# Gelu of one half times the other half, in 16 tiles: the rows that a partition owns, interleaved by tile or adjacent in memory

## The chip, the cores and the metric

The kernel runs on one core of a Trainium2 chip. The metric is the device time of a run in microseconds. The time before is the median of three runs, 470.57 us (470.28 to 470.79). A run with the hardware profiler gives the profile.

## What is computed

```
x = randn(32, 512, 2048), float32
x1, x2 = x[..., :1024], x[..., 1024:]
gelu_x1 = 0.5 * x1 * (1 + erf(x1 / sqrt(2)))
return gelu_x1 * x2          # (32, 512, 1024), float32
```

Each row of 2048 numbers (8 KB) becomes a row of 1024 numbers (4 KB). Rows don't depend on one another. There are 32 x 512 = 16,384 rows: 128 MiB (134.22 MB) are read and 64 MiB (67.11 MB) are written.

## The kernel before

The rows are flattened to one list of 16,384 and cut into 16 tiles of 1024 rows. In a tile each of the 128 partitions holds R = 8 rows. L38 and L39 set which rows these are: the list is split as (n p r), so tile n takes 1024 adjacent rows, partition p of it the eight adjacent rows from n x 1024 + p x 8 on. A tile of the input is thus 8 MB of adjacent memory, in which partitions lie 64 KB apart, and a tile of the output 4 MB with partitions 32 KB apart. Each partition's share of a tile is one unbroken piece.

SBUF holds two input tiles (`x_tiles`, L44) and two output tiles (`o_tiles`, L45), used in turn by even and odd tiles. The order of the work is written out by hand:

- `load(i)` (L54 to L59) is issued from ScalarE's queue, one DMA of 8 MB for a tile. Tile 0 alone comes in two DMAs, of rows 0 to 3 and 4 to 7 of each partition. Loads 0 and 1 are issued ahead of the loop (L61, L62).
- For each tile ScalarE applies Gelu in place to the first half of each row (L72), and VectorE multiplies it by the second half into the output tile (L77). Tiles 1 to 14 do this in one instruction each, over 128 x 8192 numbers. The first and the last tile do it in three pieces, of 2, 2 and 4 rows for each partition.
- The result goes out from SyncE's queue: one DMA of 4 MB (L89), or for the first and the last tile two DMAs of 2 MB (L87).
- At the end of the loop's body, load i + 2 is issued (L93) into the buffer that tile i has just used. It waits for the multiply of tile i.

`no_wait` (L47) tells the framework that a dependence is already implied by another wait; it adds no instruction. So there are two DMA queues, ScalarE's with the loads (q10 in the profile) and SyncE's with the stores (q1). Both are worked off by the same 16 DMA engines of the core. ScalarE also computes, so a load that waits for its buffer stands in ScalarE's order ahead of the next Gelu.

Of the kernel before, what the change touches and what calls it, by code (L numbers as in the profile page):

```python
# [1 line left out]

# [4 lines left out]

GELU = mybir.ActivationFunctionType.Gelu


@with_exitstack
def kernel(
    ctx: ExitStack,
    tc: tile.TileContext,
    x: bass.AP,
    out: bass.AP,
):

    nc = tc.nc
    P = nc.NUM_PARTITIONS  # L30

    x_flat = x.flatten_outer_dims()
    out_flat = out.flatten_outer_dims()
    n_rows, dim = x_flat.shape
    half = dim // 2

    R = 8
    x_t = x_flat.rearrange("(n p r) d -> n p r d", p=P, r=R)  # L38
    o_t = out_flat.rearrange("(n p r) d -> n p r d", p=P, r=R)  # L39
    n_tiles = x_t.shape[0]  # L40

    xpool = ctx.enter_context(tc.tile_pool(name="xpool", bufs=1))
    opool = ctx.enter_context(tc.tile_pool(name="opool", bufs=1))
    x_tiles = [xpool.tile([P, R, dim], x.dtype, name=f"x{k}_tile") for k in range(2)]  # L44
    o_tiles = [opool.tile([P, R, half], out.dtype, name=f"o{k}_tile") for k in range(2)]  # L45

    def no_wait(ins, others):  # L47
        for other in others:
            tc.declare_no_dep(ins, other, reason="implied by another wait")

    x_users, o_users = ([], []), ([], [])
    loads = {}

    def load(i):  # L54
        x_tile = x_tiles[i % 2]
        loads[i] = []
        for rows in (slice(0, 4), slice(4, 8)) if i == 0 else (slice(0, 8),):
            dma = nc.scalar.dma_start(out=x_tile[:, rows, :], in_=x_t[i][:, rows, :])  # L58
            loads[i].append(dma.ins)  # L59

    load(0)  # L61
    load(1)  # L62
    for i in range(n_tiles):
        x_tile, o_tile = x_tiles[i % 2], o_tiles[i % 2]
        last = i == n_tiles - 1
        pieces = i == 0 or last
        steps = ((0, 2), (2, 4), (4, 8)) if pieces else ((0, 8),)
        gelus, muls = [], []
        for lo, hi in steps:
            rows = slice(lo, hi)  # L70
            gelu = tc.keep_in_program_order(
                nc.scalar.activation(  # L72
                    out=x_tile[:, rows, :half], in_=x_tile[:, rows, :half], func=GELU
                )
            )
            no_wait(gelu.ins, x_users[i % 2])
            mul = nc.vector.tensor_mul(  # L77
                out=o_tile[:, rows, :],
                in0=x_tile[:, rows, :half],
                in1=x_tile[:, rows, half:],  # L80
            )
            no_wait(mul.ins, loads[i] + x_users[i % 2] + o_users[i % 2])
            gelus.append(gelu.ins)
            muls.append(mul.ins)
            if pieces and hi % 4 == 0:
                part = slice(hi - 4, hi)
                nc.sync.dma_start(out=o_t[i][:, part, :], in_=o_tile[:, part, :])  # L87
        if not pieces:
            nc.sync.dma_start(out=o_t[i], in_=o_tile)  # L89
        x_users[i % 2].extend(gelus + muls + loads[i])  # L90
        o_users[i % 2].extend(muls)
        if i + 2 < n_tiles:
            load(i + 2)  # L93


# [1 line left out]
_INS = ['x']  # L97
_OUTS = [((32, 512, 1024), 'float32')]


# [23 lines left out]
```

## Time and profile before

| what | value |
|---|---|
| median of three runs | 470.57 us (470.28 to 470.79) |
| the profiled execution's own time | 470.61 us |
| its span, from first to last instruction | 468.8 us |
| Gelu over a whole tile, L72, x14 | 7.03 us each |
| multiply over a whole tile, L77, x14 | 8.69 us each |
| a load DMA of 8 MB, from issue to landing, median | 42.2 us |
| a store DMA of 4 MB, from issue to landing, median | 42.4 us |

How to read the profile: the page gives each engine's busy time and its share of the span, then the span in 40 slices with the busy share of the 16 DMA engines in tenths and the rate that they moved in GB/s. For each DMA queue it gives the number of packets, the MB and the time that its packets took, as a share of the time of 16 engines. The chain of waits is followed back from the last instruction: each piece has its start, its length and what it was. A window is a stretch of the span with what each engine did in it. ACT is ScalarE, DVE VectorE, SP SyncE, and L72 is line 72 of the kernel.

### The profile page before, as it was taken

How to read it: one execution, taken by the hardware profiler on the slowest of the kernel's cores; microseconds unless marked ns; L12 is line 12 of the kernel's file. 1: busy time of each engine (PE TensorE's matmuls, PEld its weight loads, DVE VectorE, ACT ScalarE, POOL GpSimd, SP SyncE). 2: the span in 40 equal slices, each digit the busy share in tenths (PEclk: the TensorE clock that was granted, in tenths of full speed). 3: DMA queues.
4: the chain of work that ended last, by engine and by line, in shares of the span. 5: the costliest groups of instructions: out<-in, count | busy, mean ns of one | idle time of the engine just before them, and what ended most of it. 6: DMA issues, size and time to landing. Idle time of an engine off the chain costs nothing.

```text
span 468.8 us, 150 instructions
## 1 busy us (share of the span) xinstructions
DVE 139.5 (30%) x20; ACT 114.2 (24%) x21; POOL 0.2 (0%) x4
## 2 busy tenths in 40 slices
DVE  0330333407033070430704207052070510606142
ACT  1320505041050410505005050140501405023060
POOL 0000000000000000000000000000000000000000
DMA  8999999999999999999999999999999999999998
GB/s 358 447 447 447 414 389 495 403 403 447 481 414 403 447 403 492 403 433 417 492 403 403 447 492 403 403 447 447 447 403 439 411 492 403 403 447 492 403 403 358
DMA packets 5041, 201.33 MB, mean 429 GB/s; under 512 B 561, under 2 KB 561, under 8 KB 561
## 3 DMA queue, kind: packets, MB, share of 16 engines
q10 hardware_dynamic: 2448, 134.22, 66.3%
q1 hardware_dynamic: 2592, 67.11, 33.2%
q14 instruction: 1, 0.00, 0.0%
HBM read 134.22 MB, written 67.11 MB: 429 GB/s over the span
## 4 chain that ended last, share of the span: by engine, by line
DMA 72%; DVE 14%; ACT 12%; ACTq 1%; issue 0%
DMA x_tile<-in_x_dram 72%; DVE o_tile L77 14%; ACT x_tile L72 12%; ACTq L119 0%; ACTq L58 0%
## 5 line engine op out<-in xcount | busy, mean ns | idle before, releaser
L77 DVE TENSOR_TENSOR o_tile<-x_tile 128x8192 f32<-128x8192 f32 (+2 forms) x20 | 139.5, 6985 | 320.7 <-ACT x_tile L72 320.7
L72 ACT ACTIVATE x_tile<-x_tile 128x8192 f32<-128x8192 f32 (+2 forms) x20 | 113.0, 5662 | 339.4 <-DMA x_tile<-in_x_dram 339.4
L72 ACT ACT_TABLE_LOAD x1 | 1.3, 1283 | 2.1 <-issue 2.1
L108 POOL MEMSET const-bfloat16-1.0<- 128x1 bf16 x1 | 0.1, 102 | 0.0
L108 POOL MEMSET const-uint8-127<- 128x1 uint8 x1 | 0.1, 102 | 0.0
L108 POOL MEMSET const-float32-0.0<- 128x1 f32 x1 | 0.1, 99 | 0.2 <-issue 0.2
L108 POOL MEMSET const-float32-1.0<- 128x1 f32 x1 | 0.1, 99 | 0.0
## 6 DMA issues: line engine op xcount, KB each, us to landing
out_dram<-o_tile SPq DMA_DIRECT2D x14, 4096.0 KB, 42.4
x_tile<-in_x_dram ACTq DMA_DIRECT2D x2, 4096.0 KB, 16.8
out_dram<-o_tile SPq DMA_DIRECT2D x4, 2048.0 KB, 18.0
x_tile<-in_x_dram ACTq DMA_DIRECT2D x15, 42.2
```

The source lines that it names most:

```text
L72: nc.scalar.activation(out=x_tile[:, rows, :half], in_=x_tile[:, rows, :half], func=GELU)
L77: mul = nc.vector.tensor_mul(out=o_tile[:, rows, :], in0=x_tile[:, rows, :half], in1=x_tile[:, rows, half:],)
L108: nc = _bacc.Bacc("TRN2", target_bir_lowering=False, num_devices=1)
```

## The change

```
-    x_t = x_flat.rearrange("(n p r) d -> n p r d", p=P, r=R)
-    o_t = out_flat.rearrange("(n p r) d -> n p r d", p=P, r=R)
+    x_t = x_flat.rearrange("(p n r) d -> n p r d", p=P, r=R)
+    o_t = out_flat.rearrange("(p n r) d -> n p r d", p=P, r=R)
```

The list of rows is now split as (p n r): partition p owns the 128 adjacent rows from p x 128 on, and tile n takes eight of them from each partition, those from p x 128 + n x 8 on. A partition's share of a tile is still one unbroken piece of 64 KB in the input and 32 KB in the output. The pieces of neighbouring partitions now lie 1 MB apart in the input and 512 KB apart in the output, where they were 64 and 32 KB apart and touched one another. From tile to tile, each partition's piece moves on by 64 KB in the input and 32 KB in the output. Input and output use the same split, so each result goes to the row it came from. Nothing else in the kernel differs; its lines stand two lines lower, because two blank lines were added (the load's L58 is L60, the Gelu's L72 is L74, the multiply's L77 is L79, the stores' L87 and L89 are L89 and L91).

## The prediction, made before the changed kernel was run

> **What bounds the kernel now.** I read the page first, for busy shares and queues. Its engine table and the row of slices under it say at once which resource is full.
>
> ```profile
> span 468.8 us, 150 instructions
> ...
> DVE 139.5 (30%) x20; ACT 114.2 (24%) x21; POOL 0.2 (0%) x4
> ...
> DMA  8999999999999999999999999999999999999998
> GB/s 358 447 447 447 414 389 495 403 403 447 481 414 403 447 403 492 403 433 417 492 403 403 447 492 403 403 447 447 447 403 439 411 492 403 403 447 492 403 403 358
> ...
> q10 hardware_dynamic: 2448, 134.22, 66.3%
> q1 hardware_dynamic: 2592, 67.11, 33.2%
> ...
> HBM read 134.22 MB, written 67.11 MB: 429 GB/s over the span
> ```
>
> The two computing engines work 30% and 24% of the time; the DMA engines are full in every slice but the first and the last. The queue rows price the two directions. Loads (q10) hold 0.663 x 468.8 = 310.8 us of all 16 engines, stores (q1) 0.332 x 468.8 = 155.6 us, together 466.4 us. Only 468.8 - 466.4 = 2.4 us of the span is not covered by them. So 134.22 MB / 310.8 us = 432 GB/s and 67.11 MB / 155.6 us = 431 GB/s: both directions move at one speed, 27 GB/s for each engine.
>
> The GB/s row has a second message. A slice is 468.8 / 40 = 11.72 us. If all 16 engines finish one 32 KB packet in a slice, that is 16 x 32,768 B / 11.72 us = 44.7 GB/s. Most slices are whole multiples of it: 358 is 8, 403 is 9, 447 is 10, 492 is 11. The 16 engines therefore end their packets nearly together: they walk through their partitions' rows in step.
>
> Next the windows of the trace, to see whether the edges or the middle matter. The columns are the stretch, its length, the three engines' busy time, clock, DMA share and rate.
>
> ```profile
> 0.70:13.00 12.30, 0.00 (x0) 1.41 (x2) 0.00 (x0) 1.00 0.94 384
> 158.40:187.40 29.00, 8.69 (x1) 7.03 (x1) 0.00 (x0) 1.00 1.00 434
> 187.40:216.40 29.00, 8.69 (x1) 7.04 (x2) 0.00 (x0) 1.00 1.00 434
> ```
>
> In the middle a tile costs 29.0 us at DMA share 1.00 and 434 GB/s. The first 12.3 us run at 384 GB/s and lose 12.3 x (1 - 384/433) = 1.4 us. Last the chain and the waits, for what stands beside the transfers.
>
> ```profile
> 174.20 42.17 DMA x_tile<-in_x_dram
> 216.37 0.02 issue
> 216.39 7.04 ACT x_tile L72
> 223.43 0.02 issue
> 223.45 8.70 DVE o_tile L77
> 232.15 0.02 issue
> 232.17 42.26 DMA x_tile<-in_x_dram
> ```
>
> ```profile
> ACT x_tile L72 <- DMA x_tile<-in_x_dram: 339.4, 17, 22.0
> DVE o_tile L77 <- ACT x_tile L72: 320.7, 18, 23.6
> ```
>
> A buffer's round is 42.2 + 7.04 + 8.70 = 58.0 us for two tiles. Its load is in flight for 42.2 of 58.0 us, and there are two buffers, so 2 x 42.2 / 58.0 = 1.45 loads are in flight on average: the load queue never runs dry while the activation and the multiply hold one buffer. The activation waits 22.0 us for data in each round of 29 us. The chain names a single buffer's order; the limit under it is how fast 16 busy engines move bytes.
>
> **What the Trainium skill says.** First, DMA: Bandwidth & Descriptors, section Where 436 GB/s comes from: the ports through which the 16 engines reach SBUF add up to 435.2 GB/s. The trace agrees: 434 in the middle windows. So HBM is not what limits now. Second, the HBM Reference, section Specifications (TRN2): a pair of cores shares about 716 GB/s. One core runs here and draws 434, so by that figure 282 GB/s are spare; no run here shows the 716. Third, DMA: Bandwidth & Descriptors, section Latency and other measured facts, row "HBM row pitch at large powers of two": copies from HBM to HBM of 128 partitions x 16 KiB ran, per direction, at 207 GB/s for a pitch of 512 KiB, 164 at 2 MiB, 103 at 4 and 8 MiB, and at 214 ("full") once the pitch was off the power of two by 4 KiB. The page calls its cause, streams in step that fall on the same HBM channels, an inference. The trace of before shows the "in step" half (the multiples of 44.7) but has pitches of 64 and 32 KB alone, and there no loss. Fourth, the same page, section The descriptor swizzle: an engine serves groups of four neighbouring partitions. By that, two neighbouring engines read 4 x 64 KB = 256 KB apart now and 4 x 1 MB = 4 MB apart after; no view of this trace shows it.
>
> **The change, part by part.** Both edits are in the address patterns of L38 and L39. No instruction is added, removed or moved: the changed program has the same 17 loads, 20 activations, 20 multiplies and 18 stores in the same order on each queue. A partition's share of a tile stays one piece, 8 rows x 8 KB = 64 KB for a load and 8 x 4 KB = 32 KB for a store, so packets keep number and size (2448 and 2592). No wait is added, none goes away. Issue cost, activation (7.03 us) and multiply (8.69 us) read SBUF, which is laid out as before: 0. What is new is where the 128 pieces of a DMA lie.
>
> *Stores*: pitch 32 KB to 512 KB. The trace has no such pitch. Least cost 0 (HBM has slack); a gain is excluded, since the engines already run at the port rate. The page's price for the same pitch is 214/207 = 1.034, which I take: 155.6 x 0.034 = 5.3 us.
>
> *Loads*: pitch 64 KB to 1 MB. Least cost 0 again. The page has no 1 MiB; its neighbours are 1.034 (512 KiB) and 214/164 = 1.305 (2 MiB), that is 310.8 x 0.034 = 10.5 us to 310.8 x 0.305 = 94.8 us. From the one to the other the loss grows ninefold, so I place 1 MiB midway by factors, not by differences, and take the geometric mean of the two losses, sqrt(0.034 x 0.305) = 0.10: 310.8 x 0.10 = 31.6 us. It is an estimate from that page, carried over from HBM-to-HBM copies to copies with SBUF on one side. The total through HBM is alike (2 x 214 = 428 there, 434 here), which is my reason to carry it; that reads here come in turns with all 16 engines on one tensor could make it worse.
>
> Nothing hides either sum. The engines are at share 1.00, so each microsecond of longer packets is a microsecond of the end; the activation's and the multiply's waits of 22 us only grow. In the profiled execution: 310.8 + 31.6 + 155.6 + 5.3 + 2.4 = 505.7 us of span, and 1.8 us around it (470.61 - 468.8): 507.5. That execution is within 0.05 us of the median of 470.57, so the same number stands for the median.
>
> **The rivals.**
>
> *No change (not slower).* The mechanism is HBM's slack: place, the 16 engines' packets; price 0; it decides as long as HBM can hand each engine 27 GB/s at these addresses, 434 GB/s in all. For it: the port rate binds now, the equal 432 and 431 GB/s show no trace of HBM in either direction, and pieces of 64 KB are four times as long as the page's 16 KiB, so engines jump less often. Against: the page lost 3% at 512 KiB with about the same total, and the engines walk in step. Time 470.6, from 469.7 to 471.5.
>
> *A small loss.* The page's 512 KiB price or less, for both directions: up to 310.8 x 0.034 + 5.3 = 15.8 us, 471.5 to 486.4.
>
> *Collapse.* If the page's figures are caps for one direction, a load queue held to 207 GB/s needs 134.22 MB / 207 = 648 us, with the stores beside it: about 652 with the edges of 4.2 us. For it: in a turn of loads all 16 engines pull from one tensor at 434. Against: the page itself adds two directions to 414 through the same HBM. Everything above 570.7 belongs here.
>
> *Faster.* Only the 1.4 us of the ramp and the 2.4 us of edges could shrink, and a different layout of addresses has no reason to shorten them.
>
> *The change doesn't do what it says.* Excluded by the patterns: with p outermost the step is 16,384 / 128 = 128 rows, 128 x 8 KB = 1 MB and 128 x 4 KB = 512 KB.
>
> **How the numbers follow.** The page's price in between (486.4 to 470.6 + 94.8 + 5.3 = 570.7, point 507.5): 0.47. No change: 0.26, as the trace shows only slack. A small loss: 0.13. Collapse: 0.11. Faster: 0.03. The range from 469.7 to 570.7 leaves out collapse and faster, 0.14; leaving out no change as well would leave out 0.40. The likeliest case alone is 486.4 to 570.7. About 0.2% (0.9 us) is what a measurement here can tell from nothing, so: faster 0.03, same 0.26, slower 0.47 + 0.13 + 0.11 = 0.71.
>
> **What would show it right or wrong.** Right: the rate of the middle windows falls from 434 to 434 x 470.6/507.5 = about 400 with the DMA share still near 1.00; q10's share of the 16 engines' time rises against q1's (342.4 and 160.9 us); a load lands in some 46 us in place of 42.2; activation and multiply stay at 7.03 and 8.69. If the middle stays at 434 and 29.0 us per tile, the pitch price of the page does not hold here and HBM's slack decided. If q1 grows as much as q10, the loss does not follow the pitch as I have it. If slices stop being multiples of one packet step, the engines have fallen out of step, which would explain a smaller loss. A rate near 300 means collapse. The forecast is wrong altogether if a page's measurement between HBM tensors says nothing on copies to SBUF.

## The result and the profile after

The changed kernel takes 515.39 us (median of six runs, 513.18 to 519.06) against 470.68 us for the kernel before in the same job (470.28 to 470.86). The ratio is 1.0962, with a 95% interval of 1.0920 to 1.1004: 44.7 us slower, where 36.9 was forecast. The profiled execution took 513.18 us, of which 511.4 are its span. In all ratios of this document a run more than 1.5% above the fastest of the same kernel is left out as slow, which concerns one run at half the pitch and two at 1 MB less 1 KB.

First the page of the changed kernel.

```profile
span 511.4 us, 150 instructions
...
DVE 139.5 (27%) x20; ACT 114.2 (22%) x21; POOL 0.2 (0%) x4
...
DMA  8999999999999999999999999999999999999977
GB/s 341 425 382 309 313 399 336 367 379 418 377 413 405 415 390 405 418 413 392 410 413 405 415 408 425 413 405 408 423 413 408 420 400 408 423 397 420 413 310 318
...
q10 hardware_dynamic: 2448, 134.22, 68.0%
q1 hardware_dynamic: 2592, 67.11, 30.5%
...
HBM read 134.22 MB, written 67.11 MB: 394 GB/s over the span
```

Gelu and multiply have the same busy time to a tenth of a microsecond, packets the same number and bytes. What grew is the time that the load packets took: 0.680 x 511.4 = 347.8 us of the 16 engines, against 310.8. The stores' packets took 0.305 x 511.4 = 156.0, against 155.6. Third, 511.4 - 347.8 - 156.0 = 7.6 us are covered by neither, against 2.4. So the 42.6 us of longer span are 37.0 (loads) + 0.4 (stores) + 5.2 (engines without work).

The GB/s row shows two more things. Four of the slices 3 to 7 (counted from 0; they lie between 38 and 102 us) run at 309 to 367 GB/s; later ones stay near 410. And a step of 32 KB on all 16 engines would now be 16 x 32,768 B / 12.785 us = 41.0 GB/s, but 418, 405, 415, 390 and most others are no multiples of it: the engines no longer end their packets together.

Windows of the same trace (columns as in the prediction: stretch, length, busy time of three engines, clock, DMA share, GB/s), and the last 23.4 us of the kernel before:

```profile
31.90:55.10 23.20, 0.00 (x0) 0.00 (x0) 0.00 (x0) 1.00 1.03 340
158.40:187.40 29.00, 8.69 (x1) 4.60 (x2) 0.00 (x0) 1.00 0.99 394
...
300.00:400.00 100.00, 26.07 (x3) 21.44 (x4) 0.00 (x0) 1.00 1.00 413
488.00:511.40 23.40, 8.92 (x3) 7.22 (x3) 0.00 (x0) 1.00 0.71 302
```

```profile
445.40:468.80 23.40, 8.92 (x3) 7.22 (x3) 0.00 (x0) 1.00 0.89 381
```

The DMA share is at 1.00 while the rate is 340 to 413 in place of 434: the engines are occupied, but each packet holds them longer. In the last 23.4 us the share is 0.71. In the kernel before it was 0.89, which puts 23.4 x (0.89 - 0.71) = 4.2 of the 5.2 us there: some engines finish their part earlier than others, and the end waits for the last. The kept trace, which lists the start, length and size of every packet, bears this out. Each DMA ends with 16 packets of 4 bytes, read here as one for each engine; the time from the first of them to the last is the spread of the engines. For the last load it is 11.9 us, where it was 0.36 before.

The chain gives the growth over time. Its rounds run from the end of one multiply to the end of the next on the same buffer. Four of their loads, first in the changed kernel and then the same four in the kernel before:

```profile
70.91 49.97 DMA x_tile<-in_x_dram
...
136.69 47.61 DMA x_tile<-in_x_dram
...
385.14 45.69 DMA x_tile<-in_x_dram
...
446.64 44.44 DMA x_tile<-in_x_dram
```

```profile
62.95 37.41 DMA x_tile<-in_x_dram
...
116.17 42.22 DMA x_tile<-in_x_dram
...
348.24 42.24 DMA x_tile<-in_x_dram
...
406.29 42.24 DMA x_tile<-in_x_dram
```

The lag is 8.0, 20.5, 36.9 and 40.4 us: about half of the loss is there after a good quarter of the run. The last round shown is 446.64 - 385.14 = 61.5 us long, 3.5 over the 58.0 that a round took before, for two tiles. The waits say where it surfaces:

```profile
ACT x_tile L74 <- DMA x_tile<-in_x_dram: 382.0, 17, 27.7
DVE o_tile L79 <- ACT x_tile L74: 363.2, 18, 30.3
```

Gelu waits 42.6 us more for its data than before (339.4), which is the whole growth of the span.

### The profile page after: what moved, and what is told of

The parts are those of the page before. It is cut to its first block, busy times and chain, and to the rows that moved or that the text cites. A ratio compares the mean times of both kernels' runs of the same rounds, so it can differ in the third digit from the quotient of the medians.

```text
span 511.4 us, 150 instructions
## 1 busy us (share of the span) xinstructions
DVE 139.5 (27%) x20; ACT 114.2 (22%) x21; POOL 0.2 (0%) x4
## 4 chain that ended last, share of the span: by engine, by line
DMA 68%; DVE 14%; ACT 11%; another core or an unknown queue 4%; ACTq 0%; issue 0%
DMA x_tile<-in_x_dram 68%; DVE o_tile L79 14%; ACT x_tile L74 11%; ACTq L121 0%; ACTq L60 0%
## 5 line engine op out<-in xcount | busy, mean ns | idle before, releaser
L79 DVE TENSOR_TENSOR o_tile<-x_tile 128x8192 f32<-128x8192 f32 (+2 forms) x20 | 139.5, 6985 | 363.2 <-ACT x_tile L74 363.2
L74 ACT ACTIVATE x_tile<-x_tile 128x8192 f32<-128x8192 f32 (+2 forms) x20 | 113.0, 5662 | 382.0 <-DMA x_tile<-in_x_dram 382.0
## 6 DMA issues: line engine op xcount, KB each, us to landing
out_dram<-o_tile SPq DMA_DIRECT2D x14, 4096.0 KB, 46.2
x_tile<-in_x_dram ACTq DMA_DIRECT2D x15, 46.2
```

The lines of the kernel that those rows point to most:

```text
L74: nc.scalar.activation(out=x_tile[:, rows, :half], in_=x_tile[:, rows, :half], func=GELU)
L79: mul = nc.vector.tensor_mul(out=o_tile[:, rows, :], in0=x_tile[:, rows, :half], in1=x_tile[:, rows, half:],)
```

## The experiments

The theory after the result: the loads' pitch of 1 MB, a power of two, slows the read packets, most of all while the 16 engines walk in step. The rivals: that the stores' pitch is the cause, that distance or ownership of adjacent rows costs by itself, and that certain addresses are slow.

### Which of the two edits: loads or stores

Loads alone:

```
 x_t = x_flat.rearrange("(p n r) d -> n p r d", p=P, r=R)
-o_t = out_flat.rearrange("(p n r) d -> n p r d", p=P, r=R)
+o_t = out_flat.rearrange("(n p r) d -> n p r d", p=P, r=R)
```

> Loads at a pitch of 1 MB, stores at 32 KB as in the kernel before; the rows of the output are therefore permuted. Theory (the loss is the loads' alone): 515 us as after, within 3; load queue 340 to 350 us of the 16 engines, stores 156. Rival (the stores' pitch of 512 KB disturbs the loads, which then only show it): 471 to 480.

Stores alone, the same edit on the line of x_t instead:

> Stores at a pitch of 512 KB, loads at 64 KB as in the kernel before; the rows of the output are therefore permuted. Theory (writes don't feel the pitch): 470.6 us, within 1, every tile 29.0 us. The page's price for 512 KiB, as in the prediction: 476. Rival (the stores' pitch disturbs the loads): 490 to 515.

Measured: 506.52 us with the loads' edit alone (ratio 1.0765, 1.0738 to 1.0791), 470.87 with the stores' alone (1.0004, 0.9996 to 1.0013). The queues of the kernel with the loads' edit alone:

```profile
q10 hardware_dynamic: 2448, 134.22, 67.6%
q1 hardware_dynamic: 2592, 67.11, 30.9%
```

Its slices:

```profile
GB/s 343 416 407 372 359 428 395 403 400 400 411 403 400 395 395 403 413 408 421 411 416 413 411 390 411 411 421 413 379 416 408 398 434 405 403 416 408 408 304 322
```

Of its span of 504.3 us the load packets take 340.9, the stores 155.8, and 7.6 are covered by neither. The stores' pitch costs nothing that can be measured alone, as the theory had it, and not the 476 us of the price for 512 KiB. But the theory expected 515 for the loads alone, and 8.9 us are missing: the stores' pitch does cost, only when the loads have theirs, and it is paid in the loads' packets (347.8 against 340.9 us in the profiled runs, whose spans differ by 7.1). The slices show when: slices 3, 4 and 6 (from 0) stood at 372, 359 and 395 GB/s, where the changed kernel's stood at 309, 313 and 336.

### Which pitch: the power of two or the distance

Half the pitch, in two halves of the list:

```
+x_t = x_flat.rearrange("(m p n r) d -> m n p r d", p=P, r=R, n=8)
+o_t = out_flat.rearrange("(m p n r) d -> m n p r d", p=P, r=R, n=8)
 ...
+n_tiles = x_t.shape[0] * x_t.shape[1]
 ...
```

> Each partition owns 64 adjacent rows in each half of the list: loads at a pitch of 512 KB, stores at 256 KB, output as the reference. Theory with the page's price (512 KiB costs the loads 3.4%): 481 us. Rival 1 (any large pitch costs what 1 MB costs): 510 to 515. Rival 2 (nothing below 1 MB): 471.

Measured 473.88 us (1.0069, 1.0052 to 1.0086); three of the four runs took 473.74 to 473.99 us, the fourth 489.51. The queues of the profiled run, whose span is 472.0 us:

```profile
q10 hardware_dynamic: 2448, 134.22, 66.1%
q1 hardware_dynamic: 2592, 67.11, 33.0%
```

The load packets take 0.661 x 472.0 = 312.0 us, 0.4% more than before; the 3.4% that the prediction took from the Trainium skill for 512 KiB isn't reached. Its time without work is 472.0 - 312.0 - 155.8 = 4.2 us. Both rivals fall too: it costs 3 us, neither nothing nor 40. So a power of two does not cost much by itself: 512 KB is one, and 1 MB costs over ten times as much.

Then the load's pitch a little under 1 MB, with the stores as in the changed kernel:

```
-x_t = x_flat.rearrange("(p n r) d -> n p r d", p=P, r=R)
+x_t = [
+    bass.AP(x_flat.tensor, x_flat.offset + i * R * dim, [[127 * dim, P], [dim, R], [1, dim]])
+    for i in range(n_rows // (P * R))
+]
 ...
+n_tiles = len(x_t)
```

> Loads at a pitch of 127 rows, 1016 KB, in place of 128 rows; they read partly the same rows twice and leave some out, so the output is of other rows. Stores as after. Theory (the power of two makes the streams fall on the same places of HBM): 470.6 to 473 us. Rival (large distance between pieces costs by itself): 510 to 515.

With `128 * dim - 48` as the first step:

> Loads at a pitch of 1 MB less 192 B[...]; the pieces are shifted, so the output is of other numbers. Stores as after. The page's finding for +192 B: no help, 510 to 520 us. Rival (any break of the power of two suffices): 471.

With `128 * dim - 256`:

> Loads at a pitch of 1 MB less 1 KB[...]; the pieces are shifted, so the output is of other numbers. Stores as after. Theory (what has to differ is more than the engines drift apart by themselves, so a few KB for each partition): a part of the loss is left, 480 to 500 us. Rival (1 KB is enough): 471. Rival (nothing under 4 KB helps): 510.

With `128 * dim - 1024`:

> Loads at a pitch of 1 MB less 4 KB, the amount that the page gives as enough; the output is of other numbers. Stores as after. Theory and page: 471 us, as with 8 KB less. Rival (only whole rows of 8 KB help): 490 or more.

| loads' pitch | us | ratio, 95% interval |
|---|---|---|
| 1 MB (the changed kernel) | 515.39 | 1.0962 (1.0920 to 1.1004) |
| less 192 B | 510.26 | 1.0853 (1.0798 to 1.0907) |
| less 1 KB | 477.14 and 480.29 | 1.0170 (1.0131 to 1.0209) |
| less 4 KB | 473.75 | 1.0065 (1.0050 to 1.0080) |
| less 8 KB | 470.86 | 1.0012 (1.0002 to 1.0023) |

With 1 KB less the executions differ: two more took 485.63 and 489.21 us, so that the median of all four is 482.96. With 8 KB less, 17 of twenty runs took 470.69 to 471.07 us and three 473.5 to 473.8. The GB/s row of the kernel with 8 KB less:

```profile
GB/s 358 447 447 447 430 374 492 402 402 447 481 414 402 447 414 481 402 436 414 492 402 402 447 481 414 402 447 414 481 402 422 428 492 402 402 447 486 408 402 358
```

The pieces are as far apart as ever, to within 1%, and the loss is gone; the multiples of one packet step (402, 447, 492) are back. So distance is not the cause, the alignment to 1 MB is. The loss fades over a few KB for each partition: 192 B takes off some 5 us of 45, 1 KB most, and 4 KB leaves 3 us, where none was expected. Of those 3 the load packets hold hardly any (0.659 x 472.1 = 311.1 us against 310.8): here too it is time without work, 472.1 - 311.1 - 155.8 = 5.2 us against 2.4. The engines' spread at the last load fits: 3.7 us, against 0.46 with 8 KB less.

### Certain addresses, or being in step

The changed kernel with `x_t[n_tiles - 1 - i]` and `o_t[n_tiles - 1 - i]`, the tiles in reverse:

> The changed kernel with its tiles in reverse order, 15 first; output as the reference. Theory (the slow stretch early in the changed kernel, slices 3 to 7, is the engines walking in step until collisions spread them): 515 us, with the slow slices again early in the run. Rival (the tiles at those addresses are slow ones): 515 us, with the slow slices near the end.

Measured 517.60 us (1.1013, 1.0966 to 1.1061). Its row of slices:

```profile
GB/s 338 443 349 303 309 327 343 386 388 403 396 388 414 388 393 388 398 416 401 401 414 398 411 411 406 401 419 401 398 411 411 414 416 396 408 396 419 406 260 325
```

The slow stretch is early again, 303 to 386 in slices 3 to 7, though these are now the last tiles' addresses. Slow addresses are out.

Then kernels in which each load starts anew on all engines, with one input buffer:

```
-x_tiles = [xpool.tile([P, R, dim], x.dtype, name=f"x{k}_tile") for k in range(2)]
+x_tiles = [xpool.tile([P, R, dim], x.dtype, name=f"x{k}_tile") for k in range(1)]
 ...
-load(1)
 ...
-    if i + 2 < n_tiles:
-        load(i + 2)
+    if i + 1 < n_tiles:
+        load(i + 1)
```

> The changed kernel with one input buffer, so that each load starts alone with all 16 engines at once, after 16 us without a load; output as the reference. The kernel of before with one buffer should take about 740 us (a load of some 31 us beside its store, then 16 us of Gelu and multiply, 16 times). Theory (in step the loss is largest, as in the early slices, where the rate fell to 310 GB/s): 80 to 110 us above that, so about 830. Rival (the loss is the same whether or not the engines have spread, as in the later slices at 410 GB/s): 20 to 30 us above, about 765.

The same with (n p r) in both lines:

> The kernel of before with one input buffer; output as the reference. It is the base for the changed kernel with one buffer. Both theories: about 740 us, with the DMA engines idle during Gelu and multiply.

And with (p n r) for the loads and (n p r) for the stores:

> The changed kernel with one input buffer and stores at 32 KB; the rows of the output are permuted. With both pitches large it took 884.5 us, a load landing in 41.1 us; the layout of before took 749.5 and 32.1. Theory (while the engines are in step the stores' pitch of 512 KB makes the loads' loss worse, which is the 9 us between the two kernels with two buffers): a load lands in 35 to 39 us, 790 to 850 us in all. Rival (the stores' pitch plays no part in step): 880 to 890.

Measured: 884.52 us with the change, 749.47 without it, 843.03 with the loads' edit alone. The load's rows of the three pages, in that order (KB left out by the page, then the median from issue to landing):

```profile
x_tile<-in_x_dram ACTq DMA_DIRECT2D x15, 41.1
```

```profile
x_tile<-in_x_dram ACTq DMA_DIRECT2D x15, 32.1
```

```profile
x_tile<-in_x_dram ACTq DMA_DIRECT2D x15, 38.6
```

A load that starts anew loses 41.1 - 32.1 = 9.0 us to the change, and 15 x 9.0 = 135 us is the whole difference of the two kernels (884.52 - 749.47 = 135.1). In the later rounds with two buffers it was 3.5 / 2 = 1.75 us for a tile. The theory's 80 to 110 us was too little, the rival's 20 to 30 far too little: the same addresses cost five times as much when the engines are set going together for each tile. The stores' pitch is part of it: with stores at 32 KB the loss is 6.5 us for a load, so 2.5 us of the 9.0 come from the stores' addresses while loads and stores start together. Loads and stores set out together here and are in flight together in the middle of the two-buffer kernels too, so that alone doesn't make the difference.

The views don't tell packets by engine, but the packets of the kept traces speak for the theory. The spread of the engines is 0.3 to 0.5 us at every load of the kernel before, and 0.3 to 0.7 with 8 KB less. In the changed kernel it grows from 1.3 us at tile 0 over 6.6 at tile 2 and 9.5 at tile 4 to 11.9 at the last. With one buffer every load starts with all engines together. Its 128 packets of 64 KB, put in order of their starts and taken in eighths, have these mean lengths (us, over loads 2 to 15):

| kernel, one buffer | 1st | 2nd | 3rd | 4th | 5th | 6th | 7th | 8th |
|---|---|---|---|---|---|---|---|---|
| as changed | 4.84 | 2.95 | 3.93 | 3.06 | 3.43 | 2.77 | 2.83 | 2.47 |
| as before | 3.15 | 2.42 | 2.42 | 2.42 | 2.42 | 2.42 | 2.42 | 2.42 |

The loss is largest when the engines set out together and is nearly gone at the end of the load, when their spread is 4 to 6 us. That they collide less because they are spread is still an inference; no run sets them apart by itself.

Nor is starting together the whole condition. The load of tile 0 also starts on all engines at 1 MB, but in pieces of 32 KB and with no store beside it (the first store packet starts at 24.8 us). In the changed kernel it loses 1.2 us at its start and nothing after it, as its two halves land for the first and the third Gelu:

```profile
14.12 3.71 ACT L74 ACTIVATE x_tile<-x_tile 128x2048 f32<-128x2048 f32 x2 [10.74 <-DMA x_tile<-in_x_dram]
23.79 3.62 ACT L74 ACTIVATE x_tile<-x_tile 128x4096 f32<-128x4096 f32 x1 [5.96 <-DMA x_tile<-in_x_dram]
```

```profile
12.88 3.71 ACT L72 ACTIVATE x_tile<-x_tile 128x2048 f32<-128x2048 f32 x2 [9.49 <-DMA x_tile<-in_x_dram]
22.57 3.62 ACT L72 ACTIVATE x_tile<-x_tile 128x4096 f32<-128x4096 f32 x1 [5.98 <-DMA x_tile<-in_x_dram]
```

The second half follows the first by 9.67 us, by 9.69 before. Whether the missing stores or the shorter pieces spare this load is not shown: no run has loads of 64 KB pieces without stores.

### The same ownership without the power of two

Each partition owns 127 adjacent rows, and one row more from the last 128 of the list:

```
+x_t = x_flat[: 127 * P].rearrange("(p k) d -> p k d", p=P)
+o_t = out_flat[: 127 * P].rearrange("(p k) d -> p k d", p=P)
 ...
+def spans(i, lo, hi, flat, own):
+    end = min(i * R + hi, 127) - i * R
+    yield slice(lo, end), own[:, i * R + lo : i * R + end, :]
+    if end < hi:
+        yield slice(end, hi), flat[127 * P :].rearrange("(p k) d -> p k d", p=P)
 ...
```

> Each partition owns 127 adjacent rows and one of the last 128, so the pitches are 1016 KB and 508 KB; the last tile has one more load and one more store of one row for each partition. Output as the reference. Theory (the power of two alone is the fault of the changed kernel): 470.5 to 472 us. Rival (adjacent rows for a partition cost by themselves): 500 or more.

Measured 476.82 us (1.0130, 1.0104 to 1.0156): 39 us better than the changed kernel, 6 us behind the kernel before, outside what the theory expected. The windows say where:

```profile
145.00:261.00 116.00, 34.79 (x5) 28.12 (x4) 0.00 (x0) 1.00 1.00 434
...
435.00:476.10 41.10, 11.60 (x4) 7.32 (x3) 0.00 (x0) 1.00 0.78 336
```

The middle is back at 434 GB/s, so adjacent rows for a partition cost nothing there. The end is at share 0.78, and the timeline has the reason, in the last tile's third Gelu (the bracket is its idle time):

```profile
460.64 3.62 ACT L81 ACTIVATE x_tile<-x_tile 128x4096 f32<-128x4096 f32 x1 [8.41 <-DMA x_tile<-in_x_dram]
```

It waits 8.4 us for the small load of the odd row, 1 MB in pieces of 8 KB. That landed at 460.6, 12.1 us after the load of seven rows that was issued just ahead of it (448.5). If each of an engine's eight small packets (8 KB at 27 GB/s, 0.30 us) has to let one store packet of 32 KB pass (1.21 us), that makes 8 x 1.51 = 12.1 us. The packets of the kept trace agree: the small ones start in steps of 1.51 us, with store packets of 1.21 us on the other queue in the meantime. A version with the odd row in the first tile, where no store is in flight, was not tried.

## Why the prediction was right, point by point

The mechanism held: a larger pitch makes load packets longer, and with full engines nothing hides it. The point, 507.5 us, was 7.9 us under the 515.39 measured, and part of that nearness is luck: a store term of 5.3 us that did not come true stood where a term of 5.2 us was missing, and the loads' price was built on a neighbour that does not hold here.

- *DMA engines full, so longer packets are a longer run*: right. Gelu's waits grew by 42.6 us, as the span did; nothing hid any of it.
- *The pitch prices apply to copies with SBUF on one side*: right in kind. The 1 MB pitch costs, 4 KB off the power of two frees nearly all of it and 192 B little. This agrees with the Trainium skill (DMA: Bandwidth & Descriptors, section Latency and other measured facts, row "HBM row pitch at large powers of two"), which has full rate with 4 KiB of padding and no help from 192 B, at a pitch of 4 MiB and between HBM tensors. No change, the rival with 0.26, is refuted: whatever slack HBM has in total did not help, since the loss is one of alignment, not of bytes for each second.
- *Loads, 31.6 us*: measured 37.0 in the changed kernel, and 340.9 - 310.8 = 30.1 with the loads' edit alone. The size between the two neighbours on that page of the skill was near, but the lower neighbour itself, 3.4% at 512 KiB, was too dear for this kernel: 0.4% was measured. With that figure in its place the same mean would be sqrt(0.004 x 0.305) = 0.035, an estimate of 10.9 us. Nor is the price one number, as the sum has it: it falls during the run, and a load that starts anew pays 9.0 us where one in a late round pays 1.75.
- *Stores, 5.3 us*: wrong as a term. Store packets take 156.0 us in place of 155.6, and the stores' edit alone costs nothing that can be measured. The stores' pitch cost 8.9 us (515.39 - 506.52) in another place, as longer load packets and only beside the loads' pitch. I had summed two prices that are not independent.
- *Edges, 2.4 us as before*: wrong. They became 7.6 us, since the engines no longer finish together (a spread of 11.9 us at the last load). This term was missing; with it and the loads' 5.4 us more, less the stores' 4.9, the span comes out 5.7 us over the 505.7 that was forecast.
- *In step*: the spread of 0.3 to 0.5 us bears out the reading of the slices (a load packet of 64 KB is two of its steps, a store packet of 32 KB one), and what was named as a sign of a smaller loss happened: the multiples vanished, and the loss for two tiles fell to 3.5 us. With each load started anew, the kernel loses 135 us.
- *Signs named*: middle windows about 400 (394 to 413), a load landing in 46 us (46.2), compute unchanged, all held; q1 at 160.9 did not.

## What to carry to other kernels

When DMA engines are full, look at where the 128 pieces of one DMA lie, not only at how long they are: a pitch of 1 MB between partitions, with pieces of 64 KB and the stores at 512 KB, cost 9.6%, and with 8 KB off the loads' pitch at most 0.2%. In the profile the sign is a DMA share of 1.00 with a falling rate and unchanged packets. In a pipeline without pauses the loss shrank while the engines drifted apart; the kernel that starts each load anew paid 18% (884.52 against 749.47).

## What the runs showed that I had not expected

- Writes with a pitch of 512 KB run at full rate by themselves (470.87 us), yet make loads at 1 MB slower by 8.9 us with two buffers and by 41.5 us (884.52 - 843.03) when every load starts anew. What reads and writes share there is open.
- A loss that is largest early, once loads and stores run side by side, and heals in part: 340 GB/s from 32 to 55 us, 413 from 300 to 400 us (434 before), with nothing changed in the program.
- Engines that are only slightly out of step leave an uneven end: with 4 KB off the pitch the load packets are back to 311.1 us, but the engines end the last load 3.7 us apart, and 5.2 us without work stay where 2.4 were.
